# Encoder layer on one core: products with V placed behind the scores of a later item, and maxima sent through DRAM from GpSimd

## The chip, the cores and the metric

The kernel runs on one core of a Trainium2 chip. The metric is device time in microseconds (us) of that core for one execution. Its engines are TensorE (PE in the rows; PEld is its loading of weights), VectorE (DVE), ScalarE (ACT), GpSimd (POOL) and SyncE (SP), which only issues transfers. Each engine works through its own list of instructions in order and waits by semaphores for the others.

## The reference

One encoder layer, applied with the same weights to a prompt of 2048 rows and a sample of 512 rows, 1024 wide:

```python
h = rmsnorm(x, g_pre) * (1.0 + scale[:, None, :]) + shift[:, None, :]
proj = h @ w_in                    # qa ka va ga | qb kb vb gb
# A: 8 heads of 64; three dilated windows (128,1), (512,4), (2048,16), mixed by their softmax sums
ya = dilated_mixture(qa, ka, va).reshape(bn, s, A_WIDTH) * jax.nn.silu(ga)
# B: 4 heads, two softmax maps each, a = p0 - lam * p1, o = a @ v, rmsnorm per head
yb = diff_attention(qb, kb, vb, lam, g_sub, lam_init).reshape(bn, s, B_WIDTH) * jax.nn.silu(gb)
y = jnp.concatenate([ya, yb], axis=-1) @ w_out
return x + gate[:, None, :] * rmsnorm(y, g_post)
```

## The kernel before

All products are made of fp16 pieces: a number is split into a high and a low half, and three products (high by high, high by low, low by high) stand for one. A scale, a power of two, goes with each operand, and it comes from the operand's largest absolute value.

The work is cut into eight **units**, alternately of mixer B (one of its heads) and of mixer A (two of its heads): B, A, B, A, B, A, B, A. A unit goes over five **chunks** of 512 rows, p0 to p3 of the prompt and s of the sample. A chunk of B is four **items** (128 queries against all keys, two softmax maps), a chunk of A eight (two heads, four blocks of 128 queries each). Into the items of a chunk `interleave` weaves **fill**: the projections of the next chunk and of the next unit (`qg_proj`, lines 546 and 569, and `kv_proj`, line 472), scalings of later weights, and in the last unit the output projection (`out_proj`, line 941).

An item goes through a pipeline that `run_items` writes out:

- `front`: TensorE writes scores into PSUM tiles `sc` (three of them, of 1024 columns). A prompt item of B has four such tiles: two halves of the keys for map 0, then two for map 1, each of four products (lines 616 and 622). VectorE takes the running minimum (line 625), ScalarE the exponentials (line 637). At the end VectorE joins the two maps into `pp` (line 656), ScalarE makes the fp16 high half `hl` (line 658), and SP issues its transposition into `at` (line 659).
- `tail1`, one item later: GpSimd makes the low half of B (line 666), SP issues its transposition into `at` (line 667). For A both halves are made here (lines 770 and 772, transposed by 773 and 774).
- `tail2`: the products of the transposed weights `at` with V into PSUM tile `pv`, of which there is one (B: 48 products, line 678; A: lines 790 and 796, once for four items).
- `tail3`: the result scaled, turned by TensorE (B, line 703) and stored as `y`.

`front` pauses at two marks. At "mid" (B: behind the scores of map 0; A: behind all scores) the loop runs `tail2` of the item two back and `tail1` of the one before; at "late" (the front's end) `tail3` of B's item two back. A scheduler then settles each engine's order from the dependences, the order of the program and durations that it assumes; no edge ties the products with V to the scores beside them.

A scale needs a maximum over all 128 partitions. `allmax_slow` writes a column of 128 numbers to DRAM (`amd`), reads it back as a row on every partition (`amr`), and VectorE reduces the row (line 194). It is called 13 times: for seven weight blocks, for `w_out`, and for the `y` of each of the five chunks in the last unit. SP issues both transfers, in one list with every other transfer of the kernel.

Of the kernel before, what the change touches and what calls it, by code (L numbers as in the profile page):

```python
# [2 lines left out]

# [16 lines left out]
P = 128  # L20
# [17 lines left out]
def hybrid_kernel(ctx, tc, x_p, x_s, w_in, w_ada, w_out, cvec, cols, lamv, gsub,  # L38
# [148 lines left out]
    def allmax_slow(col):  # L187

        d = dr.tile([P, 1], F32, tag=nm("amd"), name=nm("amd"))
        nc.sync.dma_start(d, col)  # L190
        row = T(tn, [P, P], F32, "amr", bufs=2)
        nc.sync.dma_start(row, d.rearrange("p o -> (p o)").partition_broadcast(P))
        m = T(tn, [P, 1], F32, "amc", bufs=2)
        V.reduce_max(m, row, axis=AX.X)
        return m
# [394 lines left out]

    class ItemB:
        def __init__(self, r, g, c, j, st):
            self.a = r, g, c, j, st
# [1 line left out]
        def front(self):  # L598
# [9 lines left out]
            for m in range(2):  # L608
                nb = T(tn, [P, 2], F32, "nb")
                pss = []  # L610
                for hf in range(NH):
                    ps = PT([P, PS["w"]], "sc")
                    pss.append(ps)
                    for n in range(HW // 512):
                        t = hf * 8 + n * 4
                        mm(ps[:, n * 512:(n + 1) * 512], lhsT=Qc[:, j, m, 0, :], rhs=K[:, t:t + 4, m, :],  # L616
                           start=True, stop=False)

                    for n in range(HW // 512):
                        t = hf * 8 + n * 4  # L620
                        x = slice(64 * n, 64 * n + 64) if ROWS[r] else slice(0, P)
                        mm(ps[:, n * 512:(n + 1) * 512], lhsT=Qc[x, j, m, 1, :], rhs=K[x, t:t + 4, m, :],  # L622
                           start=False, stop=True)

                    V.tensor_scalar(ps[:, :HW], ps[:, :HW], u["nsc"], nb[:, 0:1] if hf else 3e38,  # L625
                                    op0=ALU.mult, op1=ALU.min, accum_out=nb[:, hf:hf + 1])
                    yield 0.43 * (HW // 512)
                nbs = T(tn, [P, 1], F32, "nbs")
                if m == 0:
                    act(nbs, nb[:, NH - 1:NH], AF.Identity, bias=lnS)  # L630
                else:
                    nbs = nb[:, NH - 1:NH]
                if m == 0:
                    yield "mid"
                for hf in range(NH):
                    pt[m, hf] = T(pp, [P, 1024], F32, "pp")
                    act(pt[m, hf][:, :HW], pss[hf][:, :HW], AF.Exp, scale=-1.0, bias=nbs,  # L637
                        accum_out=Z[:, 2 * m + hf:2 * m + hf + 1])
# [28 lines left out]
                nc.sync.dma_start_transpose(out=self.al[:, hf * 8:hf * 8 + HW // P, :], in_=lo[:, :HW])  # L667
            yield 0.0

        def tail2(self):  # L670
            r, g, c, j, st = self.a
            u = U[r, g]
            NT = SQ[r] // P
# [1 line left out]
            po = PT([P, 512], "pv")  # L675
            for i, (a, b) in enumerate(((self.ah, 0), (self.ah, 1), (self.al, 0))):
                for k in range(NT):
                    mm(po[:, :128], lhsT=a[:, k, :], rhs=Vv[:, k, 128 * b:128 * b + 128],  # L678
                       start=(k == 0 and i == 0), stop=(k == NT - 1 and i == 2))
                    if k % 4 == 3:  # L680
                        yield 0.23
            if j == 0:
# [33 lines left out]
    class ItemA:  # L716
        def __init__(self, r, g, c, h, bb, st):
            self.a = r, g, c, h, bb, st

        def front(self):  # L720
            r, g, c, h, bb, st = self.a
# [17 lines left out]
            kw = K[:, h, :, 32 * b:32 * b + 64].rearrange("p j (w u) -> p w j u", w=2)  # L739
            for s in range(2):  # L740
                for j in range(4):
                    mm(ps[32 * j:32 * j + 32, m1], lhsT=Qc[:, j, h, s, 32 * bb:32 * bb + 32], rhs=kw,  # L742
                       start=s == 0, stop=s == 1)
            yield 0.22
            sb = self.sb = T(pp, [P, 1024], F32, "pp")
            nb = T(tn, [P, 2], F32, "nb")
# [27 lines left out]
            nc.sync.dma_start_transpose(out=st["al", h][:, bb], in_=lo[:, :NA])  # L774
            yield 0.0

        def tail2(self):
            r, g, c, h, bb, st = self.a
            if bb != 3:
                return  # L780
# [6 lines left out]
            for j in range(4):  # L787
                for kc in range(NKC):
                    for i, a in enumerate((ah, al)):
                        mm(pj[:, j], lhsT=Vv[:, 4 * (k0 + kc) + j, 128 * h:128 * h + 128],  # L790
                           rhs=a[:, :, kc, 32 * j:32 * j + 32], start=(j == 0 and kc == 0 and i == 0), stop=False)
                yield 0.11 * NKC
            for bb in range(4):
                for w in range(2):
# [28 lines left out]
    def run_items(its):  # L823

        for it in its:
            p1 = PIPE[-1] if PIPE else None
            p2 = PIPE[-2] if len(PIPE) > 1 else None
            front = it.front() if it else iter(("mid", "late"))
            for x in front:
                if x == "mid":  # L830
                    if p2:
                        yield from p2.tail2()
                    if isinstance(p2, ItemA):
                        yield from p2.tail3()
                    if p1:
                        yield from p1.tail1()
                elif x == "late":
                    if isinstance(p2, ItemB):
                        yield from p2.tail3()
                else:  # L840
                    yield x
            PIPE.append(it)
# [216 lines left out]
    for n, g in enumerate(ORDER):  # L1059
# [3 lines left out]
        for i, (r, c) in enumerate(SBS):  # L1063
# [43 lines left out]
            if g2 is None and i >= 1:  # L1107
                fl.append(upto(outp, OPC[i]))
                fc += OPC[i]
            main = run_items(items(r, g, c) + ([None, None] if n + 1 == NU and i + 1 == NS else []))  # L1110
            if g >= 4:
                mc = MCF[r == "p"] * 4 * (1.55 * SQ[r] / 512 + 0.15)
            else:
# [93 lines left out]
```

## Time and profile before

| | us |
|---|---|
| runs: median of 3 (lowest to highest) | 2334.36 (2332.07 to 2337.26) |
| profiled execution | 2329.01 |
| its span, first to last instruction | 2327.2 |
| TensorE busy in the span | 1941.2 |
| VectorE, ScalarE, GpSimd busy | 1433.3, 1159.6, 689.3 |

The span is the part of the profiled execution that the trace covers. Busy time counts instructions in flight; products overlap, so a busy TensorE need not be at its peak. The granted clock of TensorE, a share of its full 2.4 GHz, was 0.929 over the span.

### The profile page before, as it was taken

How to read it: one execution, taken by the hardware profiler on the slowest of the kernel's cores; microseconds unless marked ns; L12 is line 12 of the kernel's file. 1: busy time of each engine (PE TensorE's matmuls, PEld its weight loads, DVE VectorE, ACT ScalarE, POOL GpSimd, SP SyncE). 2: the span in 40 equal slices, each digit the busy share in tenths (PEclk: the TensorE clock that was granted, in tenths of full speed). 3: DMA queues.
4: the chain of work that ended last, by engine and by line, in shares of the span. 5: the costliest groups of instructions: out<-in, count | busy, mean ns of one | idle time of the engine just before them, and what ended most of it. 6: DMA issues, size and time to landing. Idle time of an engine off the chain costs nothing. (4 is left out here: it accounts for less than half of the span.)

```text
span 2327.2 us, 47751 instructions
## 1 busy us (share of the span) xinstructions
PE 1941.2 (83%) x18506; PEld 1300.9 (56%) x18506; DVE 1433.3 (62%) x3224; ACT 1159.6 (50%) x2361; POOL 689.3 (30%) x1273
## 2 busy tenths in 40 slices
PE   5878887898788878896888878887888886999898
PEld 2665565566655556675555556674556553444343
DVE  3756777766577666666566676566676554444443
ACT  3545665555456655454456655553566643333321
POOL 1124554411135554010345442111355440000000
PEclk7899999999999998998999989999899987999999
DMA  7576668789657677777466777888678669545453
GB/s 304 171 220 141 141 136 166 163 150 184 146 129 140 148 151 168 149 167 165 100 124 135 163 148 152 173 177 232 115 156 167 147 165 179 114 106 128 111 154 118
DMA packets 730580, 361.00 MB, mean 155 GB/s; under 512 B 641888, under 2 KB 690416, under 8 KB 726896
## 3 DMA queue, kind: packets, MB, share of 16 engines
q1 hardware_dynamic: 730352, 357.94, 69.5%
q8 instruction: 145, 2.38, 0.5%
q14 instruction: 83, 0.68, 0.1%
HBM read 165.64 MB, written 36.98 MB: 87 GB/s over the span
## 5 line engine op out<-in xcount | busy, mean ns | idle before, releaser
L472 PE MATMUL pj<-w,h 128*128 128x256 f16 x3840 | 481.3, 282 | 47.1 <-DVE V L488 16.9
L472 PEld LDWEIGHTS <-h 128*128 128x128 f16 x3840 | 379.6, 101 | 122.3 <-issue 51.3
L666 POOL TENSOR_TENSOR hl<-pp,hl 128x1024 f16<-128x1024 f32 (+1 forms) x144 | 294.6, 2058 | 149.3 <-ACT hl L658 100.6
L678 PE MATMUL pv<-V,at 128*128 128x128 f16 x3072 | 230.2, 229 | 125.2 <-DMA at<-hl 115.7
L678 PEld LDWEIGHTS <-at 128*128 128x128 f16 x3264 | 205.9, 103 | 180.1 <-DMA at<-hl 145.5
L546 PE MATMUL pj<-w,h 128*128 128x128 f16 x3840 | 270.9, 225 | 22.0 <-DVE V L488 7.7
L546 PEld LDWEIGHTS <-h 128*128 128x128 f16 x3840 | 234.9, 101 | 61.1 <-issue 45.0
L455 POOL TENSOR_TENSOR rp<-q,tab_sb 128x64 f32<-128x64 f32 x160 | 63.2, 395 | 685.3 <-ACT q L478 435.0
L625 DVE TENSOR_SCALAR_CACHE_REDUCE sc<-sc,us,nb 128x1024 f32<-128x1024 f32 x128 | 172.4, 1347 | 116.1 <-PE sc L622 106.9
L569 PE MATMUL pj<-h,w 128*128 128x512 f16 x960 | 223.6, 387 | 11.0 <-ACT q L553 11.0
L772 DVE SCALAR_TENSOR_TENSOR hl<-pp,Z,hl 128x640 f16<-128x640 f32 (+2 forms) x160 | 140.6, 885 | 139.8 <-DMA at<-hl 86.6
L625 DVE TENSOR_SCALAR_CACHE_REDUCE sc<-sc,us 128x1024 f32<-128x1024 f32 (+1 forms) x160 | 188.3, 1179 | 36.4 <-PE sc L622 36.0
L770 ACT ACTIVATE hl<-pp,Z 128x640 f16<-128x640 f32 (+2 forms) x160 | 130.0, 822 | 157.2 <-DMA at<-hl 122.2
L637 ACT ACTIVATE pp<-sc,nb 128x1024 f32<-128x1024 f32 (+1 forms) x144 | 152.3, 1062 | 95.3 <-DVE sc L625 92.1
L658 ACT ACTIVATE hl<-pp 128x1024 f16<-128x1024 f32 (+1 forms) x144 | 143.7, 1004 | 98.3 <-DVE pp L656 85.2
L616 PE MATMUL sc<-K,Qc 128*128 128x512 f16 x512 | 158.8, 390 | 24.6 <-ACT pp L637 23.4
L756 ACT ACTIVATE pp<-pp,nb 128x640 f32<-128x640 f32 (+2 forms) x160 | 131.3, 821 | 93.6 <-DVE nb L751 86.3
L656 DVE SCALAR_TENSOR_TENSOR pp<-pp,rz,pp 128x1024 f32<-128x1024 f32 (+1 forms) x144 | 174.4, 1245 | 2.0
L941 PEld LDWEIGHTS <-w 128*128 128x128 f16 x960 | 93.5, 99 | 140.5 <-issue 23.0
L569 PEld LDWEIGHTS <-w 128*128 128x128 f16 x960 | 93.4, 99 | 122.7 <-issue 26.0
L637 ACT ACTIVATE pp<-sc,nbs 128x1024 f32<-128x1024 f32 (+1 forms) x144 | 152.3, 1061 | 13.7 <-DVE masks L361 7.2
L941 PE MATMUL pj<-raw,w 128*128 128x512 f16 x480 | 122.9, 390 | 20.4 <-ACT w L917 20.0
(208 smaller groups left out, 3000.3 us busy)
## 6 DMA issues: line engine op xcount, KB each, us to landing
h<-hp SPq DMA_DIRECT2D x124, 512.0 KB, 6.0
pp<-in_x_p_dram SPq DMA_DIRECT2D x32, 512.0 KB, 5.5
raw<-in_w_in_dram SPq DMA_DIRECT2D x8, 2048.0 KB, 8.7
h<-hs SPq DMA_DIRECT2D x32, 512.0 KB, 5.5
out_dram<-pp SPq DMA_DIRECT2D x20, 512.0 KB, 3.1
at<-hl SPq DMA_TRANSPOSE x608, 3.2
hp<-h SPq DMA_DIRECT2D x4, 2048.0 KB, 13.3
yp<-yt SPq DMA_DIRECT2D x32, 256.0 KB, 2.9
```

Source lines behind the costliest of these rows:

```text
L472: mm(ps[:, jj, :], lhsT=hT[:, a, k, j * P:(j + 1) * P], rhs=w[:, k, b, :], start=(k == 0 and i == 0), stop=(k == KT - 1 and i == 2))
L546: mm(ps[:, jj, 0:128], lhsT=hT[:, a, k, j * P:(j + 1) * P], rhs=w[:, k, b, 0:128], start=(k == 0 and i == 0), stop=(k == KT - 1 and i == 2))
L569: mm(ps, lhsT=w[:, k, b, 128:256], rhs=hT[:, a, k, :], start=(k == 0 and i == 0), stop=(k == KT - 1 and i == 2))
L616: mm(ps[:, n * 512:(n + 1) * 512], lhsT=Qc[:, j, m, 0, :], rhs=K[:, t:t + 4, m, :], start=True, stop=False)
L625: V.tensor_scalar(ps[:, :HW], ps[:, :HW], u["nsc"], nb[:, 0:1] if hf else 3e38, op0=ALU.mult, op1=ALU.min, accum_out=nb[:, hf:hf + 1])
L637: act(pt[m, hf][:, :HW], pss[hf][:, :HW], AF.Exp, scale=-1.0, bias=nbs, accum_out=Z[:, 2 * m + hf:2 * m + hf + 1])
L656: V.scalar_tensor_tensor(a, a, rz[:, 1:2], pt[0, hf][:, :HW], op0=ALU.mult, op1=ALU.add)
L658: act(hi[:, :HW], a, AF.Copy)
L666: nc.gpsimd.tensor_tensor(lo[:, :HW], a, hi, op=ALU.subtract)
L678: mm(po[:, :128], lhsT=a[:, k, :], rhs=Vv[:, k, 128 * b:128 * b + 128], start=(k == 0 and i == 0), stop=(k == NT - 1 and i == 2))
L772: V.scalar_tensor_tensor(lo[:, :NA], sb[:, :NA], rz, hi[:, :NA], op0=ALU.mult, op1=ALU.subtract)
L941: mm(ps, lhsT=a[:, k, :], rhs=b, start=(k == 0 and i == 0), stop=(k == KT - 1 and i == 2))
```

## The change

1. The products with V of a B item run at "late" of the item two back instead of "mid", and their first one may be issued only behind the last score product of that item (`tc.issue_after(behind)`).
2. The products with V of A run one item later (at "mid" of the item three back, or two back where the present item is not of A), also behind the present item's last score product.
3. `tail3` of B runs one item later, ahead of the `tail2` that it now shares its place with; three empty items instead of two drain the pipeline.
4. `allmax_slow` issues its two transfers from GpSimd, and has one row buffer instead of two.

```diff
     def allmax_slow(col):
 
         d = dr.tile([P, 1], F32, tag=nm("amd"), name=nm("amd"))
-        nc.sync.dma_start(d, col)
-        row = T(tn, [P, P], F32, "amr", bufs=2)
-        nc.sync.dma_start(row, d.rearrange("p o -> (p o)").partition_broadcast(P))
+        nc.gpsimd.dma_start(d, col)
+        row = T(tn, [P, P], F32, "amr", bufs=1)
+        nc.gpsimd.dma_start(row, d.rearrange("p o -> (p o)").partition_broadcast(P))
...
-        def tail2(self):
+        def tail2(self, behind):
+
             r, g, c, j, st = self.a
...
                 for k in range(NT):
-                    mm(po[:, :128], lhsT=a[:, k, :], rhs=Vv[:, k, 128 * b:128 * b + 128],
-                       start=(k == 0 and i == 0), stop=(k == NT - 1 and i == 2))
+                    with tc.issue_after(behind) if behind is not None and i + k == 0 else nullcontext():
+                        mm(po[:, :128], lhsT=a[:, k, :], rhs=Vv[:, k, 128 * b:128 * b + 128],
+                           start=(k == 0 and i == 0), stop=(k == NT - 1 and i == 2))
...
         for it in its:
-            p1 = PIPE[-1] if PIPE else None
-            p2 = PIPE[-2] if len(PIPE) > 1 else None
+            p1, p2, p3 = ((PIPE[-k] if len(PIPE) >= k else None) for k in (1, 2, 3))
             front = it.front() if it else iter(("mid", "late"))
             for x in front:
                 if x == "mid":
-                    if p2:
-                        yield from p2.tail2()
-                    if isinstance(p2, ItemA):
-                        yield from p2.tail3()
+                    for q in (p3, p2):
+                        if isinstance(q, ItemA) and not q.done and (q is p3 or not isinstance(it, ItemA)):
+                            yield from q.tail2(getattr(it, "last", None))
+                            yield from q.tail3()
+                            q.done = True
                     if p1:
                         yield from p1.tail1()
                 elif x == "late":
+                    if isinstance(p3, ItemB):
+                        yield from p3.tail3()
                     if isinstance(p2, ItemB):
-                        yield from p2.tail3()
+                        yield from p2.tail2(getattr(it, "last", None))
```

The same wrapper stands around A's first product, and `self.last` keeps the last score product of a front.

**TensorE in a chunk of the first B unit (p3).** `Qc` holds the chunk's queries, `sc` a score tile, `pv` the result of a product with V, `at` the transposed weights. Before, behind the second of the item's four score tiles:

```order
L622 LDWEIGHTS Qc_555_3231
L622 MATMUL sc_681_4024<-K_76_443,Qc_555_3231 128x512
L622 LDWEIGHTS Qc_555_3231
L622 MATMUL sc_681_4024<-K_76_443,Qc_555_3231 128x512
L678 LDWEIGHTS at_87
L678 MATMUL pv_683_4032<-V_77_444,at_87 128x128
```

Eight of the 48 products stand ahead of the item's first score tile, 32 at this place, eight behind the third tile, with projections between. With the change, in the same item, behind the fourth score tile:

```order
L621 LDWEIGHTS Qc_555_3230
L621 MATMUL sc_689_4060<-K_76_443,Qc_555_3230 128x512
L621 LDWEIGHTS Qc_555_3230
L621 MATMUL sc_689_4060<-K_76_443,Qc_555_3230 128x512
L679 LDWEIGHTS at_87
L679 MATMUL pv_693_4072<-V_77_444,at_87 128x128
```

All 48 stand here in one piece, and the next item's first score tile follows them. The line numbers are those of the changed file.

**TensorE in the last unit (A), chunk p1.** The first products of `out_proj` (`pj` from `w`, which holds chunk p0's `y`) come behind the scores of the sixth item. Before:

```order
L742 LDWEIGHTS Qc_3943_26116
L742 MATMUL sc_4083_27056<-K_3325_22374,Qc_3943_26116 32x256
L941 LDWEIGHTS w_4058_26928
L941 MATMUL pj_4062_26936<-raw_3719_24721,w_4058_26928 128x512
L941 LDWEIGHTS w_4058_26928
L941 MATMUL pj_4062_26936<-raw_3719_24721,w_4058_26928 128x512
```

With the change, behind the scores of the seventh item:

```order
L744 LDWEIGHTS Qc_3943_26115
L744 MATMUL sc_4089_27090<-K_3325_22374,Qc_3943_26115 32x256
L793 LDWEIGHTS V_3326_22377
L793 MATMUL pv_4092_27120<-at_87,V_3326_22377 128x128
L793 LDWEIGHTS V_3326_22377
L793 MATMUL pv_4092_27120<-at_87,V_3326_22377 128x128
```

Here 47 of the 48 products with V of the chunk's first head stand ahead of the first product of `out_proj`; before, they stood behind 64 of its products.

**The maximum of a weight block, first B unit.** Before, on SP (`amd` and `amr` are the column and the row, `at<-hl` transpositions, `h` a load):

```order
L190 DMA amd_1017_6258<-ag_1014_6254 128x1
L383 DMA h_798_4767<-hp1_112 128x2048 x3
L659 DMA_TRANSPOSE at_87<-hl_731_4340 128x8x128
L506 DMA vbs0_124<-Vs_311_1790 128x2x256
L383 DMA h_798_4767<-hp1_112 128x2048
L503 DMA_TRANSPOSE Ks_310_1787<-tk_797_4761 128x2x128
L659 DMA_TRANSPOSE at_87<-hl_732_4344 128x8x128
L667 DMA_TRANSPOSE at_87<-hl_749_4451 128x8x128
L667 DMA_TRANSPOSE at_87<-hl_750_4454 128x8x128
L503 DMA_TRANSPOSE Ks_310_1787<-tk_797_4761 128x2x128
L192 DMA amr_1018_6260<-amd_1017_6258 128x128
L659 DMA_TRANSPOSE at_87<-hl_761_4491 128x8x128
```

With the change, on GpSimd (`rz` are small scalars, `rp` and `q32` a rotary embedding, `hl` the low half of an item's weights):

```order
L190 DMA amd_1023_6261<-ag_1020_6257 128x1
L648 TENSOR_SCALAR rz_698_4154<-rz_698_4154,us_78_445 128x1
L649 TENSOR_TENSOR rz_698_4154<-rz_698_4154,us_78_445 128x1
L192 DMA amr_1024_6263<-amd_1023_6261 128x128
L455 TENSOR_TENSOR rp1_795_4754<-q32_794_4750,tab_sb_103 128x64
L456 TENSOR_TENSOR rp2_796_4755<-q32_794_4750,tab_sb_103 128x4x8
```

Both left SP's list; on GpSimd the second waits for the first to land, and the rotary embedding and the low halves of the items queue behind it.

## Rows read from the trace of the kernel before

**Rows 1.** The page, part 1: busy time, share of the span, instructions.

```profile
PE 1941.2 (83%) x18506; PEld 1300.9 (56%) x18506; DVE 1433.3 (62%) x3224; ACT 1159.6 (50%) x2361; POOL 689.3 (30%) x1273
```

**Rows 2.** Windows, one a unit (B, A, B, ...): columns in the first line.

```profile
core 0: us, PE busy (x) PEld busy (x) DVE busy (x) ACT busy (x) POOL busy (x), PEclk, DMA share, GB/s
...
175.00:439.00 264.00, 220.50 (x2112) 151.40 (x2111) 194.31 (x337) 159.36 (x339) 137.03 (x211) 0.95 0.71 147
439.00:641.00 202.00, 171.92 (x2126) 131.33 (x2127) 122.39 (x365) 99.06 (x197) 27.98 (x93) 0.94 0.81 162
641.00:910.00 269.00, 226.61 (x2192) 154.96 (x2190) 191.41 (x354) 161.13 (x341) 136.22 (x210) 0.96 0.70 145
910.00:1125.00 215.00, 179.16 (x2144) 137.38 (x2142) 127.54 (x386) 101.33 (x201) 26.75 (x90) 0.90 0.74 155
1125.00:1405.00 280.00, 231.86 (x2168) 157.53 (x2166) 186.45 (x332) 157.89 (x336) 135.16 (x210) 0.93 0.68 138
1405.00:1604.00 199.00, 171.71 (x2119) 132.53 (x2118) 119.15 (x358) 98.52 (x197) 28.90 (x92) 0.95 0.83 170
1604.00:1901.00 297.00, 241.72 (x2244) 163.77 (x2245) 198.02 (x345) 167.61 (x351) 134.63 (x215) 0.93 0.73 161
```

**Rows 3.** Waits, whole span: us in total, times, longest.

```profile
DVE sc L625 <- PE sc L622: 142.8, 87, 7.3
...
PE pv L678 <- DMA at<-hl: 120.8, 66, 9.2
...
ACT hl L770 <- DMA at<-hl: 122.2, 57, 7.9
...
DVE amc L194 <- DMA amr<-amd: 104.0, 13, 16.2
...
PE pv L790 <- DMA at<-hl: 45.3, 22, 8.7
...
PE sc L616 <- ACT pp L637: 23.4, 22, 4.0
```

**Rows 4.** Timeline of TensorE in a prompt chunk of the first B unit: start, us.

```profile
305.12 0.59 PE L616 MATMUL sc<-K,Qc 128*128 128x512 f16 x2
305.64 0.39 PE L622 MATMUL sc<-K,Qc 64*128 64x512 f16 x2
...
322.01 3.78 PE L472 MATMUL pj<-w,h 128*128 128x256 f16 x33
```

**Rows 5.** Timeline at the end of that unit: 48 products with V in one piece.

```profile
406.12 2.84 PE L678 MATMUL pv<-V,at 128*128 128x128 f16 x48
```

**Rows 6.** Windows around one wait for `at` (columns as in rows 2).

```profile
212.50:216.40 3.90, 0.16 (x3) 0.16 (x4) 1.20 (x3) 3.87 (x8) 3.38 (x2) 1.00 0.60 112
216.40:219.80 3.40, 3.40 (x32) 3.01 (x30) 0.00 (x0) 0.96 (x3) 1.84 (x5) 0.51 0.96 197
```

**Rows 7.** Waits of SP, the transfer queue's own: us in total, times, longest.

```profile
SPq L192 <- DMA amd<-ag: 62.1, 10, 9.0
```

**Rows 8.** Transfers of the column: count, KB each, median us from issue to landing.

```profile
amd<-ag SPq DMA_DIRECT2D x13, 0.5 KB, 8.5
```

**Rows 9.** Timeline of the last unit, chunk p0's `y` on its way to `out_proj`.

```profile
1954.15 0.37 SPq L190 DMA_DIRECT2D amd<-ag  x1
...
1964.84 0.62 SPq L916 DMA_DIRECT2D w<-yp  x1
1965.56 0.60 SPq L192 DMA_DIRECT2D amr<-amd  x1
...
1972.72 1.03 PE L941 MATMUL pj<-raw,w 128*128 128x512 f16 x2 [19.95 <-ACT w L917]
```

**Rows 10.** Groups of instructions by shape: busy us, mean ns of one, idle before.

```profile
L666 POOL TENSOR_TENSOR hl<-pp,hl 128x1024 f16<-128x1024 f32 x128 | 274.5, 2157 | 139.4 <-ACT hl L658 94.8 <-DMA at<-hl 40.9 <-issue 2.3
...
L625 DVE TENSOR_SCALAR_CACHE_REDUCE sc<-sc,us,nb 128x1024 f32<-128x1024 f32 x128 | 172.4, 1347 | 116.1 <-PE sc L622 106.9 <-ACT ojk L687 5.1 <-ACT pp L637 1.8
...
L706 DVE SCALAR_TENSOR_TENSOR yt<-pv,gsub_sb,sg 128x512 f32<-128x512 f32 x20 | 14.9, 745 | 7.7 <-PE pv L703 7.7
```

More of the change, by code (lines that the diff above doesn't have):

```diff
@@ L1 @@
 import math
-from contextlib import ExitStack
+from contextlib import ExitStack, nullcontext
 import concourse.bass as bass
@@ L621, in front @@
                         x = slice(64 * n, 64 * n + 64) if ROWS[r] else slice(0, P)
-                        mm(ps[:, n * 512:(n + 1) * 512], lhsT=Qc[x, j, m, 1, :], rhs=K[x, t:t + 4, m, :],
-                           start=False, stop=True)
+                        self.last = mm(ps[:, n * 512:(n + 1) * 512], lhsT=Qc[x, j, m, 1, :],
+                                       rhs=K[x, t:t + 4, m, :], start=False, stop=True).ins
                     V.tensor_scalar(ps[:, :HW], ps[:, :HW], u["nsc"], nb[:, 0:1] if hf else 3e38,
@@ L718, in __init__ @@
             self.a = r, g, c, h, bb, st
+            self.done = False
         def front(self):
@@ L741, in front @@
                 for j in range(4):
-                    mm(ps[32 * j:32 * j + 32, m1], lhsT=Qc[:, j, h, s, 32 * bb:32 * bb + 32], rhs=kw,
-                       start=s == 0, stop=s == 1)
+                    self.last = mm(ps[32 * j:32 * j + 32, m1], lhsT=Qc[:, j, h, s, 32 * bb:32 * bb + 32], rhs=kw,
+                                   start=s == 0, stop=s == 1).ins
             yield 0.22
@@ L775, in tail1, with tail2 @@
             yield 0.0
-        def tail2(self):
+        def tail2(self, behind):
             r, g, c, h, bb, st = self.a
@@ L789, in tail2 @@
                     for i, a in enumerate((ah, al)):
-                        mm(pj[:, j], lhsT=Vv[:, 4 * (k0 + kc) + j, 128 * h:128 * h + 128],
-                           rhs=a[:, :, kc, 32 * j:32 * j + 32], start=(j == 0 and kc == 0 and i == 0), stop=False)
+                        with tc.issue_after(behind) if behind is not None and j + kc + i == 0 else nullcontext():
+                            mm(pj[:, j], lhsT=Vv[:, 4 * (k0 + kc) + j, 128 * h:128 * h + 128],
+                               rhs=a[:, :, kc, 32 * j:32 * j + 32], start=(j == 0 and kc == 0 and i == 0), stop=False)
                 yield 0.11 * NKC
@@ L1109, in hybrid_kernel @@
                 fc += OPC[i]
-            main = run_items(items(r, g, c) + ([None, None] if n + 1 == NU and i + 1 == NS else []))
+            main = run_items(items(r, g, c) + ([None, None, None] if n + 1 == NU and i + 1 == NS else []))
             if g >= 4:
```

## The prediction

> **What bounds the kernel now.** I read the page's busy shares first. TensorE is busy 83% of the span, VectorE 62%, ScalarE 50%, GpSimd 30% [rows 1]: TensorE sets the pace, and what can be won is its idle time, 2327.2 - 1941.2 = 386 us, and the time at its lower clock. The windows by unit show where that lies. The four B units last 264, 269, 280 and 297 us with TensorE idle for 43.5, 42.4, 48.1 and 55.3 us of them; the first three A units last 202, 215 and 199 us with 30.1, 35.8 and 27.3 us idle [rows 2]. In no B unit is VectorE, the next in line, busy for more than 74% (194.31 of 264.00). The waits then name what ends the idle time: TensorE waits for the transposed weights `at` for 120.8 us in front of B's products with V (66 waits, mean 1.8, longest 9.2) and for 45.3 us in front of A's (22 waits, mean 2.1, longest 8.7). Nothing else on TensorE comes near: for a score tile to be released by the exponentials it waits 23.4 us [rows 3]. VectorE for its part waits 142.8 us for scores, so mostly it follows TensorE and not the other way round.
>
> Such a wait costs twice. From 212.5 to 216.4 us TensorE worked 0.16 us, waiting for `at`. In the 3.4 us behind it the granted clock was 0.51, which is the lower of its two levels, 1.2 GHz [rows 6].
>
> **The change, part by part.** It adds no arithmetic: the same products, reductions and transfers are issued. What moves is their place.
>
> *B's products with V.* In the order shown, they stood ahead of the item's first score tile, behind its second and behind its third; now all 48 stand behind the fourth. Two thirds of them are thus passed by at least two score tiles and the projections beside these. A score tile takes from 305.12 to 306.03, 0.91 us; a projection product 3.78/33 = 0.115 us [rows 4], and in the order after the change 24 such products stand between the second tile and the fourth. The cover is 2 x 0.91 + 24 x 0.115 = 4.6 us. The mean wait is 1.8 us, so the ordinary wait vanishes; of the few long ones (up to 9.2 us) about half stays. I take 85% of 120.8 as removed, 103 us; the ends are 0 (the item period shrinks with the wait, and the data comes as late as before relative to it) and all 120.8.
>
> *A's products with V.* They move one item back. Forty items in the second unit's 202 us are 5.0 us each, against a mean wait of 2.1 us. With the same 85%: 38 us of 45.3; ends 0 and 45.3.
>
> *What comes back.* Of these 141 us I expect half to reappear as other waits, for three reasons. First, the 48 products in one piece take 2.84 us [rows 5], and the next item's first score tile 0.91 us behind them. VectorE's reduction of the fourth tile takes 1.347 us [rows 10], after which it has no score tile for 2.84 + 0.91 - 1.35 = 2.4 us; it can join the maps of the item meanwhile, but only once ScalarE has done two exponentials. Secondly, with TensorE faster, score tiles wait more often for ScalarE (23.4 us now). Thirdly, A's transposes are themselves late: ScalarE waits 122.2 us until a transposition has freed `hl` [rows 3], and no place on TensorE makes that shorter. The ends are nothing back and everything back; half because VectorE at 74% leaves room but not in every place. Net: -70.5 us.
>
> *The clock.* Twice the missing share times the length gives the time at the lower level: in the B units 26.4 + 21.5 + 39.2 + 41.6 us, in the A units 24.2 + 43.0 + 19.9 us, together 216 us [rows 2]. TensorE works some 80% of it at half speed, so 216 x 0.8 / 2 = 86 us are lost. A third of these stretches stand behind waits that go: -28 us, between 0 and -60.
>
> *The maxima.* SP stands 62.1 us at the second transfer until the first has landed, ten times [rows 7], and every transposition queues behind it; this goes. VectorE stands 104.0 us in 13 waits for the row [rows 3]. The column lands 8.5 us after its issue at the median, though it has only 0.5 KB [rows 8]: that time is spent behind other transfers in flight. From GpSimd the pair no longer waits for SP's list, but it waits for GpSimd's. What a GpSimd-issued transfer costs that engine, the trace doesn't show. It lies between SP's 0.37 us for an issue [rows 9] and the 2.157 us of GpSimd's largest operation [rows 10]; I take 1 us, so 26 us on an engine that is busy 30%. Behind the pair stand the rotary embedding and the low halves, whose transpositions the last third of B's products needs; the later place of these products covers it. Gain -8 us; ends -35 (VectorE's 104.0 us fall by a third, and all of that reaches TensorE) and, for the other case below, +110.
>
> The Trainium skill speaks against this part. "DMA: Bandwidth & Descriptors", section "Latency and other measured facts", gives about 0.6 us to the first byte for transfers issued from SP and about 1 us for those from GpSimd. An estimate from that page: 26 x 0.4 = 10 us more on VectorE's waits in place of a gain, which would bring the sum to 2249 us. No row here shows a transfer issued from GpSimd, so the sum stays with the rows.
>
> *The last unit.* From the issue of its column at 1954.15 chunk p0's `y` needs 18.6 us, and TensorE waits 19.95 us at `out_proj`'s first product [rows 9]. The load `w<-yp`, issued at 1964.84, is as late as the row `amr` at 1965.56, so a faster pair alone frees little; but 47 products with V now stand ahead, nearly 2.8 us. This is inside the -8.
>
> *`tail3` beside `tail2`.* There is one `pv`, so at each of 20 chunk ends of B the turned result must be read by VectorE (745 ns, [rows 10]) before the products with V may start. The fourth score tile and a few projections stand between and hide most of it; without that cover it would be 20 x 0.745 = 15 us. I take +3.
>
> **Sum.** -70.5 - 28 - 8 + 3 = -103.5 us on the profiled execution's 2329.0: 2225.5. The median of the runs lies 5.4 us above that execution, so I forecast 2231 us, 4.4% less.
>
> **The rivals.**
> *The waits only change their name* (0.20). TensorE no longer waits for `at`, but for `sc`: VectorE and ScalarE have a loop of their own through three score tiles, and that becomes the pace. For it speaks the lump of 48 products just where VectorE has finished its last tile; against it VectorE's 142.8 us of waits for scores. All 141 us come back, half of the clock's gain and the -8 stay: 2334 - 14 - 8 + 3 = 2315 us; with a quarter of the waits truly gone it is near 2285.
> *Nothing comes back* (0.06): 141 us, two thirds of the clock's loss (57) and 20 for the maxima go: 2334 - 218 = 2116 us.
> *The lump starves VectorE* (0.08, slower). In each of 64 prompt items of B, VectorE and ScalarE stand idle for the 2.84 us in which TensorE writes no scores, and the item grows by that: 64 x 2.84 = 182 us, against 141 removed, with no gain of clock: 2334 + 182 - 141 = 2375 us. It decides from 141/64 = 2.2 us an item; below that the kernel is faster. Against it: in the order before, 32 products already stood in one piece.
> *GpSimd's list is held by the pair* (0.05, slower). The second transfer waits on GpSimd for the first to land, 8.5 us 13 times, 110 us, and all that queues behind it reaches TensorE through the queries, keys and low halves of the next items, while the lump takes half of the rest: 2334 + 110 - 70.5 - 28 = 2345 us. Against it: a later place of the products covers just these low halves.
> *No effect* (0.03). The scheduler had mixed the products already and the new order merely trades; 2330 to 2339 us. Against it stands the order itself, in which every piece of 48 has moved.
>
> **How the numbers follow.** The forecast has 0.58; its own range is 2165 to 2285 us, from a quarter to three quarters coming back (plus or minus 35), and the ends of clock and maxima (plus or minus 25). The first rival fills 2285 to 2324, the second lies mostly below 2150. For 8 in 10 I take 2150 to 2320. Under 0.2% (4.7 us) is about what a measurement of this kernel can't tell from no change. Faster: 0.58 + 0.20 + 0.06 = 0.84. Same: 0.03. Slower: 0.08 + 0.05 = 0.13.
>
> **What the profile of the changed kernel would show.** If right: the waits of TensorE for `at` fall from 166 us to under 40, its idle time from 386 to some 310, the granted clock from 0.929 to above 0.94; waits for `sc` by the exponentials grow, but to less than 60 us; SP has no wait for `amd`; VectorE's 13 waits for the row stay near 100 us. The forecast is wrong if the waits for `sc` and of VectorE for scores take up what was removed, or if GpSimd shows long idle stretches in front of the second transfer with the rotary embedding late behind it; it is too small if the waits for `at` vanish and TensorE's idle time falls by over 130 us.

## The result, and the profile after

The changed kernel takes 2245.98 us (median of 4 runs, 2236.21 to 2248.76) against 2333.22 us: a ratio of 0.9626, interval 0.9581 to 0.9671. The forecast was 2231, range 2150 to 2320. The profiled execution took 2248.76 us, its span is 2247.0. The page of after, part 1, answers to [rows 1]:

```profile
PE 1924.8 (86%) x18506; PEld 1283.8 (57%) x18506; DVE 1421.3 (63%) x3224; ACT 1159.5 (52%) x2361; POOL 727.7 (32%) x1299
```

The span is 80.2 us shorter. TensorE has as many instructions as before and is busy 16.4 us less (1941.2 to 1924.8). That is about what the clock gave: by the granted clock the span holds 330 us at the lower level before (2 x 0.071 x 2327.2) and 288 after (2 x 0.064 x 2247.0), and 42 us less of half speed, with TensorE at work in some 80% of them, are 17 us. Its idle time fell by 63.8 us (386.0 to 322.2). The windows by unit, as in [rows 2]:

```profile
170.30:416.00 245.70, 218.78 (x2087) 148.03 (x2086) 181.04 (x319) 155.75 (x326) 136.01 (x202) 0.95 0.75 157
416.00:620.20 204.20, 172.88 (x2151) 129.98 (x2151) 127.24 (x393) 104.59 (x214) 35.27 (x104) 0.95 0.81 162
620.20:872.00 251.80, 222.91 (x2185) 151.47 (x2183) 187.11 (x343) 158.81 (x336) 144.00 (x212) 0.96 0.75 156
872.00:1068.20 196.20, 169.46 (x2125) 130.51 (x2124) 118.34 (x359) 98.92 (x197) 28.56 (x90) 0.95 0.81 166
1068.20:1340.00 271.80, 230.41 (x2183) 156.78 (x2184) 196.30 (x360) 160.52 (x339) 143.72 (x214) 0.91 0.70 144
1340.00:1534.10 194.10, 168.37 (x2127) 129.57 (x2126) 117.84 (x357) 98.95 (x197) 27.32 (x92) 0.96 0.82 169
1534.10:1829.30 295.20, 245.41 (x2234) 166.04 (x2234) 199.37 (x347) 166.15 (x347) 141.63 (x214) 0.88 0.76 165
```

The first two B units became 18 and 17 us shorter (264 to 245.7, 269 to 251.8), with 26.9 and 28.9 us of TensorE idle in place of 43.5 and 42.4. The third gained 8 and the fourth 2, at a granted clock of 0.91 and 0.88. The first three A units changed by +2, -19 and -5 us; in the second of them the granted clock rose from 0.90 to 0.95. TensorE's waits, to be set against [rows 3]:

```profile
PE sc L615 <- ACT pp L636: 71.3, 49, 12.1
PE pv L793 <- DMA at<-hl: 50.2, 23, 16.5
PE pj L472 <- DVE Vs L488: 27.3, 7, 11.2
PE pj L472 <- DVE V L488: 21.9, 10, 9.6
...
PE pv L679 <- DMA at<-hl: 11.1, 5, 2.8
```

B's wait for `at` all but vanished (120.8 to 11.1), A's did not (45.3 to 50.2). Waits of score tiles for the exponentials rose by 47.9 us (23.4 to 71.3), and the longest, 12.1 us, falls on one of VectorE's waits for a maximum's row. In front of `kv_proj`'s products (line 472) TensorE waits 49.2 us for VectorE to read the tile, 25 us more than before (16.9 + 7.3). VectorE's and GpSimd's waits for the maxima answer to [rows 3, 7]; SP has no wait for `amd` any more:

```profile
DVE amc L194 <- DMA amr<-amd: 109.4, 13, 12.6
POOL amr L192 <- DMA amd<-ag: 103.3, 13, 12.7
```

The transfers of the maxima, as in [rows 8] (KB each, median us from issue to landing):

```profile
amr<-amd POOLq DMA_DIRECT2D x13, 64.0 KB, 5.3
amd<-ag POOLq DMA_DIRECT2D x13, 0.5 KB, 8.3
```

What such a wait can do is seen in the timeline of after, at the start of the last B unit:

```profile
1573.34 0.65 POOL L190 DMA_DIRECT2D amd<-ag  x1 [1.66 <-DVE ag L863]
...
1575.49 2.84 PE L679 MATMUL pv<-V,at 128*128 128x128 f16 x48
...
1579.55 0.39 PE L621 MATMUL sc<-K,Qc 64*128 64x512 f16 x2
1579.87 0.39 PE L569 MATMUL pj<-h,w 128*128 128x512 f16 x1
...
1584.69 0.60 POOL L192 DMA_DIRECT2D amr<-amd  x1 [9.48 <-DMA amd<-ag]
...
1588.93 0.29 DVE L194 TENSOR_REDUCE amc<-amr 128x1 f32<-128x128 f32 x1 [11.01 <-DMA amr<-amd]
1589.33 1.34 DVE L624 TENSOR_SCALAR_CACHE_REDUCE sc<-sc,us,nb 128x1024 f32<-128x1024 f32 x1
...
1592.34 1.01 PE L615 MATMUL sc<-K,Qc 128*128 128x512 f16 x2 [12.08 <-ACT pp L636]
```

The column leaves at 1573.34, the row is reduced at 1588.93: 15.6 us. In between VectorE stands 11.01 us, since the reduction of the row is next in its list and the score tiles' minima (line 624) are behind it. TensorE has filled all three score tiles by 1579.94 and then stands 12.08 us for the exponentials, which need the minima. The products with V of this place were done at 1578.3, so they cover nothing. In the last unit TensorE's 20 us in front of `out_proj` [rows 9] are gone, and a wait of 16.48 us stands in front of A's products:

```profile
1886.21 0.65 POOL L190 DMA_DIRECT2D amd<-ag  x1 [11.95 <-DVE Z L770]
...
1891.25 1.24 SPq L776 DMA_TRANSPOSE at<-hl  x1
...
1900.73 3.59 PE L793 MATMUL pv<-at,V 128*128 128x128 f16 x32 [16.48 <-DMA at<-hl]
1901.48 0.28 DVE L194 TENSOR_REDUCE amc<-amr 128x1 f32<-128x128 f32 x1 [12.43 <-DMA amr<-amd]
```

It lies beside a maximum, but not behind VectorE's list: TensorE stands from 1884.25, before the column leaves, and goes on before the row is reduced. What it waits for is a transposition that lands late. The transpositions issued from 1886.66 to 1891.25 took 9.4 to 11.5 us to land (first line below), where the median of all `at` is 3.2 (second line):

```profile
DMA to landing us min/median/max: 9.4/10.6/11.5
DMA to landing us min/median/max: 2.3/3.2/13.5
```

### The profile page after: what moved, and what is told of

Same layout as the page of the kernel before. It is cut to its first block, busy times and chain, and to the rows that moved or that the text cites. A ratio compares the mean times of both kernels' runs of the same rounds, so it can differ in the third digit from the quotient of the medians.

```text
span 2247.0 us, 47773 instructions
## 1 busy us (share of the span) xinstructions
PE 1924.8 (86%) x18506; PEld 1283.8 (57%) x18506; DVE 1421.3 (63%) x3224; ACT 1159.5 (52%) x2361; POOL 727.7 (32%) x1299
## 5 line engine op out<-in xcount | busy, mean ns | idle before, releaser
L665 POOL TENSOR_TENSOR hl<-pp,hl 128x1024 f16<-128x1024 f32 (+1 forms) x144 | 291.8, 2043 | 109.4 <-ACT hl L657 105.8
L546 PE MATMUL pj<-w,h 128*128 128x128 f16 x3840 | 265.2, 224 | 20.0 <-ACT q L553 8.6
L679 PEld LDWEIGHTS <-at 128*128 128x128 f16 x3264 | 199.2, 102 | 35.9 <-issue 19.8
L679 PE MATMUL pv<-V,at 128*128 128x128 f16 x3072 | 198.8, 227 | 9.5 <-DMA at<-hl 8.2
L569 PEld LDWEIGHTS <-w 128*128 128x128 f16 x960 | 92.9, 99 | 125.5 <-issue 27.0
L751 DVE CUSTOM_DVE_ANT_0 pp<-sc,maskp,us 128x384 f32<-128x384 f32 (+1 forms) x128 | 85.8, 679 | 77.6 <-PE sc L744 77.3
```

The costliest lines, as they stand in the source:

```text
L546: mm(ps[:, jj, 0:128], lhsT=hT[:, a, k, j * P:(j + 1) * P], rhs=w[:, k, b, 0:128], start=(k == 0 and i == 0), stop=(k == KT - 1 and i == 2))
L569: mm(ps, lhsT=w[:, k, b, 128:256], rhs=hT[:, a, k, :], start=(k == 0 and i == 0), stop=(k == KT - 1 and i == 2))
L665: nc.gpsimd.tensor_tensor(lo[:, :HW], a, hi, op=ALU.subtract)
```

## The experiments

**One part of the change at a time.** Of the changed kernel, the products moved but the maxima back on SP:

```
-        nc.gpsimd.dma_start(d, col)
+        nc.sync.dma_start(d, col)
...
-        nc.gpsimd.dma_start(row, d.rearrange("p o -> (p o)").partition_broadcast(P))
+        nc.sync.dma_start(row, d.rearrange("p o -> (p o)").partition_broadcast(P))
```

> The products with V moved as in the change; the maxima stay on SP, with two row buffers. Theory (the gain is the wait of the products for their transposed weights, the maxima give next to nothing, since the column's landing, 8.3 us from GpSimd and 8.5 us from SP, did not change): 2240 to 2260 us, ratio to the kernel before 0.960 to 0.968, waits of TensorE for the weights in B under 20 us, VectorE's wait for the row 95 to 115 us. Rival (the maxima on GpSimd carry a share, by freeing SP's list of 62 us of standing): 2270 to 2300 us.

Measured: 2279.01 us, ratio 0.9794 (0.9768 to 0.9820): the rival's range, so the maxima carry a share. And the kernel before with only these lines changed the other way:

> The maxima issued from GpSimd alone; the products with V at their old place. Theory: within 0.4% of the kernel before (2324 to 2343 us); TensorE's wait for the weights in B stays at 110 to 130 us; SP no longer stands at the second transfer, GpSimd stands about 100 us there instead. Rival (SP's list was what made the weights late): 2295 to 2315 us and waits in B under 90 us. Second rival (GpSimd's list held by the pair delays the low halves): 2345 us or more, waits in B above 135 us.

Measured: 2320.61 us, ratio 0.9948 (0.9923 to 0.9973), a little below the 2324 expected at least. Apart the two parts give 2.06% and 0.52%, together 3.74%: 48 + 12 us against 87, so 27 us (give or take 13, by the three intervals) are there only when both are. The waits of the kernel with only the maxima moved:

```profile
PE pv L678 <- DMA at<-hl: 112.0, 70, 7.6
...
POOL amr L192 <- DMA amd<-ag: 92.9, 12, 12.5
DVE amc L194 <- DMA amr<-amd: 60.7, 11, 17.8
```

VectorE's wait is 43 us shorter than before, and the end saw 12 of it, while GpSimd stands 92.9 us at the second transfer with the low halves behind it, whose transpositions the old place of the products still needs. That the later place covers this and so makes the 27 us is argued, not shown; against it, the waits for `at` did not grow (112.0 us, 120.8 before).

**A's products back at their old place**, all else as after:

```
-                    for q in (p3, p2):
-                        if isinstance(q, ItemA) and not q.done and (q is p3 or not isinstance(it, ItemA)):
-                            yield from q.tail2(getattr(it, "last", None))
-                            yield from q.tail3()
-                            q.done = True
+                    if isinstance(p2, ItemA):
+                        yield from p2.tail2(None)
+                        yield from p2.tail3()
```

> As the change, but A's products with V stay at their old place (item two back, no tie to the scores). Theory (A's move gives nothing: its waits were 45.3 us before and 50.2 us after): 2240 to 2255 us, no difference to the changed kernel that can be measured. Rival (A's move hides waits that would have grown, as everything else became faster): 2265 us or more, waits of A's products above 70 us.

Measured: 2233.87 us, ratio 0.9609 (0.9574 to 0.9645), not to be told from after's 0.9626. A's move brought nothing to the end here: A's waits for `at` are 29.3 us in this kernel, and a wait of 21.2 us at `out_proj` is back.

**No edge**, so that the new order stands in the code, but the scheduler may place the products earlier:

```
-                            yield from q.tail2(getattr(it, "last", None))
+                            yield from q.tail2(None)
...
-                        yield from p2.tail2(getattr(it, "last", None))
+                        yield from p2.tail2(None)
```

> As the change, but without the tie that holds the first product with V behind the last score product: the scheduler mixes the products with scores again, up to half an item earlier. Theory (what counts is how late the products come): half of the gain, 2270 to 2300 us, waits for the weights in B 40 to 90 us. Rival (the place in the program alone is enough, since it is half an item later): 2240 to 2255 us. Second rival (the lump of 48 costs, mixing is better): under 2235 us.

Measured: 2282.93 us, ratio 0.9817 (0.9785 to 0.9849), half of the gain gone, as expected. The waits of TensorE moved back with it:

```profile
PE pv L679 <- DMA at<-hl: 80.7, 52, 4.7
PE pv L793 <- DMA at<-hl: 58.7, 21, 22.8
PE sc L615 <- ACT pp L636: 44.8, 39, 7.6
```

**The price of the trip through DRAM.** Both kernels with the trip left out: each partition takes its own maximum, the scales and the output differ, all else is the same.

```
-        d = dr.tile([P, 1], F32, tag=nm("amd"), name=nm("amd"))
-        nc.gpsimd.dma_start(d, col)
         row = T(tn, [P, P], F32, "amr", bufs=1)
-        nc.gpsimd.dma_start(row, d.rearrange("p o -> (p o)").partition_broadcast(P))
+        V.tensor_copy(row[:, 0:1], col)
...
-        V.reduce_max(m, row, axis=AX.X)
+        V.reduce_max(m, row[:, 0:1], axis=AX.X)
```

> The changed kernel with the trip of the thirteen maxima through DRAM left out: each partition takes its own maximum instead of the maximum over all 128, so the scales, and with them the output, differ; the rest of the work is the same. It prices all that the changed kernel still pays for the maxima. In its trace VectorE waits 109.4 us for them in 13 pieces and GpSimd 103.3 us. Theory (with the products moved, TensorE no longer stands still for other reasons while VectorE waits, so most of VectorE's wait reaches the end): 50 to 100 us less than 2246, so 2145 to 2195, and TensorE's waits for exponentials at the score tiles fall from 71 us to under 45. Rival (these waits lie beside other work; what the move of the maxima to GpSimd was worth came from SP's list alone): within 20 us of 2246, waits at the score tiles near 71.

> The kernel before with the same trip left out (each partition takes its own maximum, so the output differs). Beside the run of the changed kernel without the trip it tells whether the two parts of the change are worth more together than apart. Theory (before, TensorE's waits for the transposed weights cover a part of what the maxima cost): the gain here is clearly less than there, 20 to 50 us, so 2280 to 2312, and the difference between the two kernels without the trip is larger than the 49 to 54 us that the products alone were worth. Rival (the costs simply add): the same gain as there to 10 us; the difference stays at 50 to 55 us.

Measured: changed 2167.88 us, ratio 0.9278 (0.9235 to 0.9321); before 2240.51 us, ratio 0.9585 (0.9539 to 0.9631). The trip cost the kernel before some 94 us (2334.87 in these runs, less 2240.51) and the changed one some 78 (2245.98 less 2167.88); issued the other way it is 80 in the old order (2320.61 less 2240.51) and 111 in the moved one (2279.01 less 2167.88). The kernels were not all run beside each other; by the ratios the four prices are 97, 81, 85 and 120. For the kernel before I had expected 20 to 50: that TensorE's own waits cover a part of it is refuted. In the changed kernel the waits for exponentials fell to 59.8 us, not under 45 as expected.

The price is not VectorE's wait for the row alone. In the order of the four prices that wait is 104.0, 109.4, 60.7 and 126.8 us, in the third less than the price. To leave out the trip also takes away SP's standing for the column (62.1 us before, 87.5 with only the products moved) and the transfers themselves.

**The maxima by TensorE** in place of the trip (a transposition of the column, a maximum along the row, a product with ones):

```
-        pow2(E, S, (allmax if n == 0 else allmax_slow)(ag), f"w{g}")
+        pow2(E, S, allmax(ag), f"w{g}")
...
-        pow2(E, wo["S"], allmax_slow(ag), "wo")
+        pow2(E, wo["S"], allmax(ag), "wo")
...
-        pow2(s[:, 0:1], s[:, 1:2], allmax_slow(ag), "y")
+        pow2(s[:, 0:1], s[:, 1:2], allmax(ag), "y")
```

> The changed kernel with all maxima taken across the partitions by TensorE (a transposition of the column, a maximum along the row, a product with ones that spreads it) in place of the trip through DRAM; the output is the reference's. It asks whether the price of the trip can be had back without leaving it out. Theory: the trip's 12.6 us become some 3 us of short instructions, so most of what the kernel without the trip gains is kept, 2165 to 2215. Rival (TensorE takes its instructions in order, so it stops itself at the transposition until VectorE has made the column, with score tiles behind it): thirteen stops of 3 to 8 us, 40 to 100 us, so 2220 to 2260, no gain.

> The kernel before with all maxima taken by TensorE; the order of the products stays as before. With the changed kernel so treated (2197) it gives the worth of the moved products where no trip through DRAM is left in either. Theory (the worth of the products is 73 us when nothing waits for maxima, as between the two kernels without the trip): 2260 to 2280. Rival (TensorE's stops for the maxima would in the old order fall on waits that it has anyway, and cost nothing there): 2235 to 2255, a worth of 40 to 55.

Measured: changed 2197.32 us, ratio 0.9413 (0.9354 to 0.9472); before 2250.00 us, ratio 0.9633 (0.9597 to 0.9669). The first lies in its theory's range, the second misses its theory's 2260 to 2280 and lies in the rival's range. The old order with its maxima on TensorE is thus as fast as the whole change, and both together are 2.2% faster again. TensorE's stops of 3 to 8 us did not come; its waits for these maxima in the changed kernel:

```profile
PE pv L180 <- DVE ag L306: 9.7, 2, 8.7
PE pv L184 <- DVE am L182: 3.4, 5, 1.5
```

The 8.7 us are not new: the kernel after, whose first maximum goes this way too, has a wait of 8.9 us there. The third and fourth B unit are 25 and 22 us shorter than after's:

```profile
1074.50:1321.50 247.00, 221.77 (x2190) 151.57 (x2190) 189.91 (x343) 159.43 (x336) 139.49 (x210) 0.97 0.75 156
1522.50:1795.40 272.90, 238.08 (x2236) 161.58 (x2236) 201.76 (x348) 166.03 (x347) 142.37 (x212) 0.92 0.80 175
```

The eight kernels by how the maxima are taken, as ratios to the kernel before:

| maxima | products as before | products moved | worth of the move |
|---|---|---|---|
| DRAM, issued from SP | 1 | 0.9794 | 2.1% |
| DRAM, issued from GpSimd | 0.9948 | 0.9626 | 3.2% |
| TensorE | 0.9633 | 0.9413 | 2.2% |
| left out | 0.9585 | 0.9278 | 3.1% |

**Transfers behind a column.** The late transpositions of the last unit are not alone. In the trace of the kernel before, 12 transpositions were issued within 6 us behind a column; they landed 6.7 to 14.0 us after their issue, 8.3 at the median. In the changed kernel the median of 12 is 9.0. Over all transpositions it is 3.2 in each. With the maxima on TensorE, within 6 us behind the moment at which VectorE has a column ready, the medians are 3.4 (16, old order) and 3.2 (19, products moved). So the trip also holds up the transfers beside it, and TensorE's waits for `at` hold a part of its price: the longest of them in B before, 9.2 us [rows 3], ends with a transposition that was issued 10.8 us behind a column and took 8.4 us to land. How much of the price goes this way, and whether the column makes it alone, no run separates.

**The place of the products.** B's 48 products behind the third score tile in place of the fourth, first with the maxima as after, then with them on TensorE:

```
                     yield 0.43 * (HW // 512)
+                    if m == 1 and hf == 0:
+                        yield "pv"
...
-                elif x == "late":
-                    if isinstance(p3, ItemB):
-                        yield from p3.tail3()
-                    if isinstance(p2, ItemB):
-                        yield from p2.tail2(getattr(it, "last", None))
+                elif x in ("pv", "late"):
+                    if x == "pv" or not isinstance(it, ItemB):
+                        if isinstance(p3, ItemB):
+                            yield from p3.tail3()
+                        if isinstance(p2, ItemB):
+                            yield from p2.tail2(getattr(it, "last", None))
```

> The changed kernel with the 48 products of a B item behind the third of the later item's four score tiles in place of the fourth (the edge points at the third tile's last product). It asks where the part that came back (waits for exponentials at the score tiles 23 to 71 us) has its source. Theory of the prediction (the products lie in one piece between the scores of two items, so ScalarE's exponentials are fed in bursts): behind the third tile the fourth tile comes later and the next item's first tile follows directly, its score buffer still being read; the waits for exponentials change by over 20 us and the time by 10 to 30, which sign is open; the waits for the transposed weights rise from 11 to 20 to 60, since the products come one tile (0.9 us and its waits) earlier. Rival (what came back is the maxima's stops, whatever the place): waits for exponentials within 15 us of 71, time within 10 of 2246.

> The changed kernel with all maxima by TensorE and the 48 products of a B item behind the third score tile in place of the fourth. It repeats the trial of the place without the maxima's stops, which covered it. Theory (the waits for exponentials, 55 us there, are the third and fourth score tiles standing until one of two score buffers has been read, and the edge keeps the products behind them; one tile earlier they fill that gap): waits for exponentials fall to 25 to 45, waits for the transposed weights rise by less, time 2175 to 2195. Rival (as with the maxima by DRAM, the products then wait for the transposed weights and the fourth tile stands behind them): waits for the transposed weights in B over 30 us, time 2200 to 2225.

(There are three score tiles' buffers, not two as the second of these says: it is the fourth tile that waits for the first one's.) Measured: 2271.90 us, ratio 0.9711 (0.9667 to 0.9755), with DRAM, slower than after by 0.9%, with intervals that just touch; 2192.24 us, ratio 0.9396 (0.9359 to 0.9434), with TensorE, the same as behind the fourth tile. In both the time is the theory's, but not the waits for exponentials. The waits of the first of the two:

```profile
PE sc L615 <- ACT pp L638: 70.8, 45, 9.7
PE pv L795 <- DMA at<-hl: 46.1, 20, 14.8
PE pv L681 <- DMA at<-hl: 38.6, 22, 3.8
```

and of the second:

```profile
PE sc L615 <- ACT pp L638: 49.1, 48, 4.6
PE pv L681 <- DMA at<-hl: 37.8, 24, 4.4
```

At the earlier place B waits 38 us for `at` in either, against 10 to 11 behind the fourth tile; the waits for exponentials don't change in the first and fall from 55.4 to 49.1 in the second. So the place one tile earlier seems to lose with the trip and only trades without it.

**A's part once more, without the trip**: the maxima on TensorE and A's products at their old place, with B's behind the fourth tile and behind the third.

> The changed kernel with all maxima by TensorE and the A items' products back at their old place, two places earlier. Theory (the A part of the change, free of the maxima that fell into the other unit type, gains what its units showed, some 10 us a unit of 202 against 207): without it 10 to 30 us slower than 2197, so 2207 to 2227. Rival (A's waits for the transposed weights were never taken away, 45 us before and 50 after, so its move is worth nothing): 2190 to 2204.

> All maxima by TensorE, B's products behind the third score tile, and the A items' products back at their old place. Beside the same kernel with A's products moved (2192, ratio 0.9396) it asks once more, free of the maxima's stops, what A's part of the change is worth; the pair with B's products behind the fourth tile gave 2216 against 2197, with intervals that touch. Theory (A's move is worth some 19 us when nothing waits for maxima): 2205 to 2217, ratio 0.945 to 0.950. Rival (A's waits for the transposed weights are as long at either place, the 19 us are scatter): 2188 to 2199, ratio 0.937 to 0.943.

Measured: 2215.88 us, ratio 0.9485 (0.9442 to 0.9528), against 0.9413 with A moved, intervals that overlap; 2194.00 us, ratio 0.9395 (0.9366 to 0.9425), against 0.9396. The first is its theory's, the second its rival's. Of three pairs two show nothing and one 19 us. What that one pair shows stays open; a worth of A's move that holds in general is not there.

## Why the prediction was right, and where it was off

**The bound and the mechanism: right.** TensorE's waits for `at` in B were what a later place could remove: 109.7 us went where 103 were forecast. Without the edge 80.7 us of them stay and half of the gain is lost.

**A's 38 us: wrong.** The step took the mean wait of 2.1 us against an item period of 5.0. The waits were as long after it (50.2 us, 16.5 of them beside a maximum in the last unit), and with A left where it was the time is the same. The third reason given under *What comes back* (A's transposes are late themselves) would have spoken for zero here, and was not used.

**What comes back: about the right size, from several sources.** Idle time fell by 63.8 us, where the terms for it were -70.5 - 8 + 3 = -75.5. The cleanest pair, both with the maxima on TensorE, shows how much the lump has of it. TensorE's waits in the old order:

```profile
PE pv L678 <- DMA at<-hl: 113.7, 73, 5.3
PE sc L616 <- ACT pp L637: 24.2, 22, 3.2
```

And with the products moved:

```profile
PE sc L615 <- ACT pp L636: 55.4, 40, 3.7
...
PE pv L679 <- DMA at<-hl: 9.8, 10, 4.6
```

Here 104 us leave and 31 come back at the score tiles; another 19 come back at A's scores, which wait for their queries (12.2 to 30.9 us). In the kernel after, 48 us came back at the score tiles; the other 16 or so go with the trip, and so may the 25 us in front of `kv_proj`. The timeline of one item in the second of these kernels shows how the 31 arise:

```profile
648.81 2.34 PE L679 MATMUL pv<-V,at 128*128 128x128 f16 x39
...
650.99 0.59 PE L615 MATMUL sc<-K,Qc 128*128 128x512 f16 x2
...
652.03 1.29 DVE L624 TENSOR_SCALAR_CACHE_REDUCE sc<-sc,us 128x1024 f32<-128x1024 f32 x1 [2.15 <-PE sc L621]
...
653.95 2.54 DVE L655 SCALAR_TENSOR_TENSOR pp<-pp,rz,pp 128x1024 f32<-128x1024 f32 x2
...
656.41 1.34 DVE L624 TENSOR_SCALAR_CACHE_REDUCE sc<-sc,us,nb 128x1024 f32<-128x1024 f32 x1
...
658.17 1.11 ACT L636 ACTIVATE pp<-sc,nbs 128x1024 f32<-128x1024 f32 x1
...
659.43 1.01 PE L615 MATMUL sc<-K,Qc 128*128 128x512 f16 x2 [3.73 <-ACT pp L636]
```

While the products run, VectorE has no score tile for 2.15 us (the prediction worked out 2.4). It then takes the first tile, joins the maps of the item before, and comes to the second tile at 656.41; the first exponential waits for that one's minimum, and the fourth tile waits 3.73 us for the first one's buffer. That is the first of the three reasons, and the rival *The lump starves VectorE* in small: under 0.5 us an item (31/64), far from the 2.2 at which it would have decided.

**The clock: too large, and not where it was forecast.** -28 was forecast; TensorE's busy time fell by 16.4, and the granted clock rose from 0.929 to 0.936, not above 0.94. The prediction's own sum over the seven units gives 220 us at the lower level after, where it was 216: what the clock gave lies ahead of the first unit and in the last. The third and fourth B unit, which hold TensorE's stops of 11.2 us (in front of `kv_proj`) and 12.1 us (at a score tile) beside maxima, stand at 0.91 and 0.88; with the maxima on TensorE they stand at 0.97 and 0.92.

**The maxima: the term that was mis-sized.** -8 was forecast. On the order as it was they gave 12 us, on the moved one 33 (39 by the ratios). The step that failed is "mostly it follows TensorE": VectorE's 13 waits were taken to reach TensorE for little. A wait at the head of its list can stop TensorE as soon as three score tiles are full (VectorE stands from 1577.9 us in the timeline above, TensorE from 1580.3). That is one road of several. In VectorE's 13 waits, with the 4 us behind each, TensorE is idle for 75.1 us in the kernel before: 35.4 of them end with `at`, 18.6 at `out_proj`, and only 0.4 at a score tile. In the kernel after it is 65.9 us: 19.7 in front of `kv_proj`, 15.4 at score tiles, 13.9 with `at`. How the trip's 94 us divide between VectorE's list, SP's standing and transfers that land late stays open. GpSimd as issuer removed only a part (94 to 80 in the old order, 111 to 78 in the moved one); the trip itself is the larger cost. The prediction also put the column's 8.5 us down to other transfers in flight; no run shows that, and what the traces show is other transfers late behind a column. The Trainium skill's "DMA: Bandwidth & Descriptors", "Latency and other measured facts", spoke against the move with a later first byte from GpSimd. The column landed in 8.3 us from GpSimd against 8.5 from SP, so here that difference doesn't show, and the sum by that page (2249) is closer to the result by another road: the terms for A and the clock were too good by about what the maxima were too poor.

**`tail3` beside `tail2`:** line 679 waits 2.8 us for `yt`; +3 was forecast. **The rivals:** GpSimd is held at the second transfer for 103.3 us, as *GpSimd's list is held by the pair* said (110), and the kernel is faster all the same; the later place of B's products leaves 11.1 us of waits for `at`, so the low halves came in time. *The waits only change their name* is the case for about a third of B's; A's simply stayed.

**What the profile was to show:** waits for `at` under 40 us (61.3: A's), idle near 310 (322), clock above 0.94 (0.936), waits for exponentials under 60 us (71.3), no wait of SP for `amd` (none), VectorE's 13 waits near 100 us (109.4). The total was within 15 us because three misses offset each other, not because each term held, and that is luck. (Its own range, 2165 to 2285, should by its terms, 35 and 25 about 2231, read 2171 to 2291.)

## What to carry to other kernels

Put work that waits for a slow transfer behind the work of a later item, and hold it there with an edge: the order in the code alone gave half. Before that, price every wait at the head of an in-order engine's list by leaving the waited-for thing out: thirteen small maxima through DRAM cost more than the reordering gained, though VectorE was busy only 62% of the time. Look as well at what lands beside such a transfer: transpositions issued behind the column landed after 8 to 9 us in place of 3. Where a value must cross the partitions in the middle of a pipeline, a transposition and a product on TensorE cost 11 to 31 us here in all (0.9633 against 0.9585, 0.9413 against 0.9278), where two small transfers of some 8 and 5 us cost 78 to 111. The best version of this study, maxima on TensorE and the products moved, takes 2192 to 2197 us, 6% less than before.

## What was not expected of the hardware

An issue of a transfer costs GpSimd 0.63 us for the column and 0.56 us for the row (13 each), where 1 us was taken and SP needs 0.37 and 0.60 in one place [rows 9]. The groups of after, with busy us, mean ns of one and idle time before:

```profile
L190 POOL DMA_DIRECT2D amd<-ag x13 | 8.2, 634 | 105.4 <-DVE ag L306 42.7 <-DVE Z L770 38.6 <-DVE ag L907 17.3
L192 POOL DMA_DIRECT2D amr<-amd x13 | 7.3, 560 | 103.3 <-DMA amd<-ag 103.3
```

A column of 0.5 KB takes 7.9 to 9.5 us to land from either engine (medians of the kernels with the trip), longer than a row of 64 KB (4.7 to 5.9 us over the kernels here). Why the smaller is the slower one was not tried.
